# Whole-slot low parts, half-slot high parts, and a seventh Strassen-like slot in the first pair of the down product

## The chip, the cores and the metric

The kernel runs on one core of a Trainium2 chip. The metric is the device time of one execution in microseconds, from three runs of the kernel before; the profile is of one further execution. Four engines matter: PE (TensorE) multiplies, ACT (ScalarE) copies and rounds, DVE (VectorE) adds and subtracts, and SP (SyncE) only issues transfers from DRAM.

## The reference, cut to what matters

A decoder block on 256 tokens of width 2048, all in float32: a norm, one wide projection, two kinds of attention, two gates, an output projection, and a gated MLP with a short causal convolution.

```python
proj = rmsnorm(x, attn_norm_w) @ w_in                  # 2048 x 11264 columns
merged = sigmoid(g_ret) * (o_ret @ w_ret_up) + sigmoid(g_moba) * (o_moba @ w_moba_up)
x = x + merged @ w_out                                 # the kernel's x2
up = causal_dwconv(rmsnorm(x, ffn_norm_w) @ w_ffn_up)  # 2048 x 11264
a, b = split(up, 2)
x = x + (silu(a) * b) @ w_ffn_down                     # 5632 x 2048
return rmsnorm(x, final_norm_w)
```

## The kernel before

All weights come from DRAM once, cut into halves of 128 x 1024 float32 (512 KB). Two halves make a slot, and the kernel walks through 252 slots: those of the projection, 64 of the gates and the output projection (`middle_slots`), 88 of FFN's first product (`up`), 44 of its second (`down_slots`, "dn"), the last in two pairs of 22.

Precision is kept by splitting. Of each raw half (`raw`), ACT writes the high part `whi` (rounded to float32r), and DVE the low part `wlo = raw - whi`. A product is then three matmuls: high by high, high by low, low by high (`mm3`). The activations are split in the same way: `xb` holds those of the projection and of `up` (its tiles `xtiles`), `ot*`, `mg*`, `gh`/`gl` those of later products. In the projection's q and k groups and in `up`, the weights are the stationary operand (`wide_products`: per slot 16 matmuls of `whi` against 512 columns, then of `wlo` against 256). Elsewhere the activations are stationary and the 512 columns of weights move.

A "seven" is a slot whose 2 x 2 block product is done with seven block products in place of eight (the scheme of Strassen and Winograd): 21 matmuls of 512 columns in place of 24. It costs DVE and ACT more: four sums of raw weights and three more blocks to split (`seven_parts`, `seven_parts_apart`; tiles `tt`, `th`, `tl`, `t`), and four sums of activations, split too (`seven_sums`; tiles `room`, `s`), which both pairs of `dn` share. `SEVEN` lists which of the 22 slots in each pair of `dn` are sevens.

The order on each engine is the order of the program text: nothing is reordered, and a tool puts in the semaphores. In each slot's code first stands `part` for the next slot (ACT and DVE split it, then SP is told to load into the raw buffers that this frees), then small tasks (`run_tasks`: attention, convolution, norms), then the slot's matmuls. `RAW_BUFS` and `PART_BUFS` say how many halves of raw and of split weights fit: four each, so the splits run at most about a slot ahead of PE, and the loads two.

Of the kernel before, what the change touches and what calls it, by code (L numbers as in the profile page):

```python
# [16 lines left out]
P = 128  # L17
# [16 lines left out]
RAW_BUFS, PART_BUFS = 4, 4  # L34
# [45 lines left out]
SEVEN = ((4, 7, 10, 13, 16, 18), (3, 5, 7, 9, 12, 14, 16))  # L80
# [45 lines left out]
def block(ctx: ExitStack, tc: tile.TileContext, a):  # L126
# [32 lines left out]
    def spans(n):  # L159
        step = CW if n < 1 else 2 * CW  # L160
        return [slice(c, c + step) for c in range(0, 2 * CW, step)]

    def load(n, *some):
        if n < n_halves:
            if n not in raws:
                raws[n] = wp.tile([P, 2 * CW], F32, name="raw", bufs=RAW_BUFS)
            for w in some or spans(n):
                nc.sync.dma_start(raws[n][:, w], wts[order[n], :, w])

    def part(n, *some):  # L170

        if n < n_halves:
            if n not in parts:
                parts[n] = [wp.tile([P, 2 * CW], F32R, name=x, bufs=PART_BUFS) for x in ("whi", "wlo")]
            for w in some or spans(n):
                split2(parts[n][0][:, w], parts[n][1][:, w], raws[n][:, w])
            if not some or some[0] == spans(n)[-1]:
                raws.pop(n)
                load(n + RAW_BUFS)


# [14 lines left out]
    def mm3(out, ah, al, bh, bl, start, stop, **kw):  # L196
        mm(out, ah, bh, start=start, stop=False, **kw)
        mm(out, ah, bl, start=False, stop=False, **kw)
        mm(out, al, bh, start=False, stop=stop, **kw)

# [72 lines left out]
    xtiles = [px.tile([P, 2, 2, S], F32R, name=f"xb{i}", bufs=1) for i in range(KD // 2)]  # L273
# [18 lines left out]
    def part_x(k):  # L292
        for j in range(k, min(k + 2, KD)):
            split2(xh[j], xl[j], xts[j // 4][:, j % 4, :], vec[:, V_ATTN + j:V_ATTN + j + 1])
            if k == 0:
                part(0, spans(0)[j])
# [230 lines left out]
    def ffn(acc, f):  # L527

        pf = big["pf"]
        u = big["u"][f % 2]  # L530
        y = pf.tile([P, 2, S], F32, name="y", bufs=2)
# [12 lines left out]
        g = pf.tile([P, S], F32, name="g", bufs=2)  # L544
# [5 lines left out]
    def finish(acc, t, more):  # L550
# [17 lines left out]
        wf = big["wf"][1][:, CW:]  # L568
# [48 lines left out]
    def closed(kind, n, acc, more):  # L617
# [17 lines left out]
        elif kind == "up":  # L635
            if n == 0:
                assert not tasks, len(tasks)
                left.close()
                pf = big["pf"] = pool(left, "pf")
                big["gh"], big["gl"] = (pf.tile([P, NFB - 16, S], F32R, name="g" + x) for x in "hl")  # L640
                big["u"] = [pf.tile([P, 2, S + 2], F32, name=f"u{i}") for i in range(2)]
                for u in big["u"]:
                    nc.vector.memset(u[:, :, 0:2], 0.0)
# [12 lines left out]
    load(0)  # L656
# [8 lines left out]
    part(1)  # L665
# [12 lines left out]
    def seven_parts(n):  # L678


        r, q = raws.pop(n), raws.pop(n + 1)
        b11, b21, b12, b22 = r[:, :CW], r[:, CW:], q[:, :CW], q[:, CW:]
        (h1, l1), (h2, l2) = [[wp.tile([P, 2 * CW], F32R, name=x, bufs=PART_BUFS) for x in ("whi", "wlo")]
                              for _ in range(2)]
        (h3, l3), t2 = big["t14"], big["t2"]
        nc.scalar.activation(h1, r, AF.Copy)
        nc.scalar.activation(h2[:, CW:], b22, AF.Copy)
        nc.vector.tensor_sub(l1, r, f32(h1))
        nc.vector.tensor_sub(l2[:, CW:], b22, f32(h2[:, CW:]))
        nc.vector.tensor_sub(b11, b12, b11)  # L690
        nc.vector.tensor_sub(b12, b22, b12)
        nc.scalar.activation(h2[:, :CW], b12, AF.Copy)
        nc.vector.tensor_sub(b22, b22, b11)
        nc.scalar.activation(t2[:, 0, :], b22, AF.Copy)
        nc.vector.tensor_sub(b21, b21, b22)
        nc.scalar.activation(h3, r, AF.Copy)
        nc.vector.tensor_sub(l2[:, :CW], b12, f32(h2[:, :CW]))
        nc.vector.tensor_sub(t2[:, 1, :], b22, f32(t2[:, 0, :]))
        nc.vector.tensor_sub(l3, r, f32(h3))
        parts[n], parts[n + 1] = (h1, l1), (h2, l2)  # L700
        for i in (0, 1):
            load(n + i + RAW_BUFS)

    def seven_parts_apart(n, tt=None, t124=None):

        r, q = raws.pop(n), raws.pop(n + 1)
        b11, b21, b12, b22 = r[:, :CW], r[:, CW:], q[:, :CW], q[:, CW:]
        (h1, l1), (h2, l2) = [[wp.tile([P, 2 * CW], F32R, name=x, bufs=PART_BUFS) for x in ("whi", "wlo")]
                              for _ in range(2)]
        if t124 is None:  # L710
            splits = [(big["th"], big["tl"], big["tt"])]
            tt = [big["tt"][:, x, :] for x in range(3)]
        else:
            splits = [(*t124[x], tt[x]) for x in (1, 0, 2)]
        nc.vector.tensor_sub(tt[0], b12, b11)
        nc.vector.tensor_sub(b12, b22, b12)
        nc.vector.tensor_sub(tt[1], b22, tt[0])
        nc.vector.tensor_sub(tt[2], b21, tt[1])
        split2(h1, l1, r)
        split2(h2, l2, q)  # L720
        for hi, lo, full in splits:
            split2(hi, lo, full)
        parts[n], parts[n + 1] = (h1, l1), (h2, l2)
        for i in (0, 1):
            load(n + i + RAW_BUFS)
# [16 lines left out]
    def seven_sums(k, pool_k, tag, kind="dn"):  # L742
# [7 lines left out]
        nc.vector.tensor_sub(sums[:, 2, :], x[:, 0, :P], x[:, 0, P:])  # L750
        nc.vector.tensor_sub(sums[:, 1, :], sums[:, 0, :], x[:, 0, :P])
        nc.vector.tensor_sub(sums[:, 3, :], x[:, 1, :P], sums[:, 1, :])  # L752
        big["s", kind, k] = pool_k.tile([P, 2, 4, P], F32R, name=f"s{k}", tag=tag, bufs=1)
        hi, lo = big["s", kind, k][:, 0], big["s", kind, k][:, 1]
# [3 lines left out]
    def seven_products(xs, sums, t124, accs, halves):  # L758
# [94 lines left out]
    def middle_slots(slot):  # L853
# [4 lines left out]
        t124 = [two_of(p1.tile([P, 2, CW], F32R, name="t", tag="kq", bufs=4)) for _ in range(3)]  # L858
        for i, (seven, two) in enumerate(slots):
# [18 lines left out]
            if out and q == 3:  # L878
                right.close()
                pr = pool(right, "pr", "right")  # L880
                big["x2"] = pr.tile([P, NT, D], F32, name="x2")
# [19 lines left out]
            if i == 8:  # L901
                middle_pool()
                t124 = [[big[x][:, i, :] for x in ("th", "tl")] for i in range(3)]
            n = 2 * (slot + 1)
            if q == 0 and seven:
                times(r, sr)
            if i + 1 < len(slots) and slots[i + 1][0]:
                if i < 8:
                    tt = [p1.tile([P, CW], F32, name="tt", tag=x, bufs=2) for x in ("tmp", "tmp", "full")]
                    seven_parts_apart(n, tt, t124)  # L910
                else:
                    seven_parts_apart(n)
            else:
                part(n)
                part(n + 1)
# [9 lines left out]
            if not out:  # L925
                if c == 1 and q == 2:
                    seven_sums(3, big["pm"], "s3", "gr")
                if c == D // CW - 1 and q >= 10:
                    seven_sums(q - 10, big["pm"], f"s{q - 8}", "wo")
# [17 lines left out]
            halves = [parts.pop(2 * slot + h) for h in range(2)]  # L947
# [27 lines left out]
    def weighted(c, n):  # L975
        x3 = big["x2"][:, :, c * CW:(c + n) * CW]
        wf = big["wf"][c // 2][:, c % 2 * CW:(c % 2 + n) * CW]
        nc.vector.tensor_mul(x3, x3, wf[:, None, :].to_broadcast([P, NT, n * CW]))  # L978

    def down_slots(slot):  # L980
# [4 lines left out]
        t124 = [[x[:, :CW] for x in big["t14"]], [big["t2"][:, x, :] for x in range(2)],  # L985
                [x[:, CW:] for x in big["t14"]]]
        for i, (seven, where) in enumerate(slots):
# [8 lines left out]
            n = 2 * (slot + 1)  # L996
            if i + 1 < len(slots):
                if not slots[i + 1][0]:
                    part(n)
                    part(n + 1)  # L1000
                elif p == 0:
                    seven_parts(n)
                else:
                    seven_parts_apart(n, [big["pf"].tile([P, CW], F32, name="tt", tag=x, bufs=b)
                                          for x, b in (("u0", 1), ("u1", 1), ("y", 2))], t124)
            if p == 0 and q in SEVEN[0][:-1]:
                k = SEVEN[0].index(q) + 1
                seven_sums(k, px, f"xb{k % 5}")
            if p == 1 and q == 5:
                seven_sums(6, big["pf"], "wa")  # L1010
            if q == SEVEN[p][-1] + 1:
                v = big["pf"].tile([P, 2, S], F32, name="y", bufs=2).rearrange("p a t -> p (a t)")
                spawn(gathered, at, 2 * p, v)
            if p == 1 and q in (16, 17):
                j = q - 16
                wf = px.tile([P, 2 * CW], F32, name="wf", tag=f"xb{j + 1}", bufs=1)
                big.setdefault("wf", []).append(wf)
# [175 lines left out]
```

## Time and profile before

| what | value |
|---|---|
| median of 3 runs | 1417.61 us (1417.16 to 1417.9) |
| profiled execution, first to last instruction | 1415.7 us |
| what lies around it in a run | about 1.9 us |
| PE | 7215 matmul records, busy 99% of the span |
| DVE | busy 78% |
| ACT | busy 55% |
| DRAM read | 272.86 MB, 194 GB/s |

In the profile's groups a row has the source line, the engine, what is written and read with its shape, the number of instructions, the busy time in us and the mean of one in ns, and then the idle time just before them and what ended it. A PE record is longer (about 390 ns) than the distance to the next one, since matmuls overlap in the array; the distance is what counts. In a row of a timeline the first number is the start, the second how long the merged piece lasted.

### The profile page before, as it was taken

What the parts mean: (1) busy time and instruction counts of PE and PEld (TensorE: products, weight loads), DVE (VectorE), ACT (ScalarE), POOL (GpSimd) and SP (SyncE); (2) the same over time, 40 slices, a digit from 0 to 9 for tenths busy, and PEclk for the clock granted to TensorE, in tenths of its full rate; (3) what the DMA queues carried; (4) which work ended last, traced back from release to release, by engine and by line L of the source; (5) the groups of instructions that cost most, each with busy time, mean ns of one, the idle gap of its engine ahead of it and who ended that gap; (6) DMA issues with size and microseconds to landing.
All of it is one profiled execution on the core that took longest, in us unless ns stands there. A gap on an engine that the chain in (4) does not pass through costs nothing. (4 is left out here: it accounts for less than half of the span.)

```text
span 1415.7 us, 19297 instructions
## 1 busy us (share of the span) xinstructions
PE 1405.6 (99%) x7215; PEld 1202.7 (85%) x7215; DVE 1103.4 (78%) x1512; ACT 776.9 (55%) x1043; POOL 5.6 (0%) x14
## 2 busy tenths in 40 slices
PE   9999999999999999999999999999999999999997
PEld 7888888888888888888888888888888888888886
DVE  6687656867888989798677777777777778998886
ACT  6555454545556555555565555555555555555553
POOL 0000000000000000000000000000000000000000
PEclk9999999999999999999999999999999999999999
DMA  8755555555656656577555656556556555657664
GB/s 296 260 187 168 167 186 172 178 179 172 212 182 209 195 191 209 180 236 238 167 190 188 197 181 193 194 182 194 191 182 196 189 179 178 207 180 236 191 217 160
DMA packets 77325, 276.22 MB, mean 195 GB/s; under 512 B 8720, under 2 KB 9776, under 8 KB 77232
## 3 DMA queue, kind: packets, MB, share of 16 engines
q1 hardware_dynamic: 76800, 274.20, 60.1%
q8 instruction: 56, 0.92, 0.3%
q10 hardware_dynamic: 432, 0.79, 0.2%
q14 instruction: 37, 0.30, 0.1%
HBM read 272.86 MB, written 2.10 MB: 194 GB/s over the span
## 5 line engine op out<-in xcount | busy, mean ns | idle before, releaser
L186 DVE TENSOR_TENSOR wlo<-raw,whi 128x1024 fp32r<-128x1024 f32 (+1 forms) x493 | 584.1, 1219 | 234.7 <-ACT whi L185 108.8
L185 ACT ACTIVATE whi<-raw 128x1024 fp32r<-128x1024 f32 (+1 forms) x493 | 514.5, 1058 | 458.9 <-PE acc L194 247.9
L194 PE MATMUL acc<-xb,whi 128*128 128x512 f32 x1920 | 466.0, 392 | 1.1 <-ACT whi L185 1.1
L194 PEld LDWEIGHTS acc<-xb,whi 128*128 128x128 f32 x1920 | 350.6, 188 | 68.6 <-ACT whi L185 2.1
L194 PEld LDWEIGHTS acc<-xb,wlo 128*128 128x128 f32 x1920 | 250.9, 191 | 12.2
L194 PE MATMUL acc<-xb,wlo 128*128 128x256 f32 x1920 | 254.6, 282 | 0.0
L194 PE MATMUL acc<-whi,xb 128*128 128x512 f32 x572 | 183.3, 391 | 0.0
L194 PEld LDWEIGHTS acc<-whi,xb 128*128 128x128 f32 x572 | 107.4, 188 | 22.1
L194 PE MATMUL acc<-wlo,xb 128*128 128x512 f32 x286 | 111.5, 390 | 0.0
L194 PE MATMUL acc<-wlo,gh 128*128 128x512 f32 (+1 forms) x226 | 87.5, 387 | 0.0
L194 PE MATMUL acc<-whi,gl 128*128 128x512 f32 (+1 forms) x226 | 87.5, 387 | 0.0
L194 PE MATMUL acc<-whi,gh 128*128 128x512 f32 (+1 forms) x226 | 87.5, 387 | 0.0
L541 DVE SCALAR_TENSOR_TENSOR y<-u,vec,y 128x256 f32<-128x256 f32 x176 | 73.5, 479 | 0.0
L194 PEld LDWEIGHTS acc<-wlo,xb 128*128 128x128 f32 x286 | 53.7, 188 | 10.6
L194 PE MATMUL z<-whi,xb 128*128 128x512 f32 x156 | 51.9, 390 | 0.0
L194 PEld LDWEIGHTS acc<-wlo,gh 128*128 128x128 f32 x226 | 42.4, 188 | 8.8
L194 PEld LDWEIGHTS acc<-whi,gh 128*128 128x128 f32 x226 | 42.4, 188 | 8.7
L194 PEld LDWEIGHTS acc<-whi,gl 128*128 128x128 f32 x226 | 42.4, 188 | 8.6
L538 ACT ACTIVATE y<-u,vec 128x256 f32<-128x256 f32 x88 | 47.7, 590 | 0.0
L194 PEld LDWEIGHTS z<-whi,xb 128*128 128x128 f32 x156 | 29.3, 188 | 6.1
L755 ACT ACTIVATE s<-room 128x512 fp32r<-128x512 f32 x13 | 8.2, 633 | 44.7 <-DVE room L752 44.7
L534 DVE TENSOR_TENSOR u<-y,r2b 128x512 f32<-128x512 f32 x44 | 30.5, 693 | 1.5
(304 smaller groups left out, 1593.1 us busy)
## 6 DMA issues: line engine op xcount, KB each, us to landing
raw<-in_wts SPq DMA_DIRECT2D x503, 512.0 KB, 4.3
rows<-in_x SPq DMA_DIRECT2D x4, 512.0 KB, 7.7
x<-in_x SPq DMA_DIRECT2D x4, 512.0 KB, 6.1
xt<-in_xT SPq DMA_DIRECT2D x3, 512.0 KB, 7.0
wf<-in_wf SPq DMA_DIRECT2D x2, 512.0 KB, 7.1
out<-x SPq DMA_DIRECT2D x4, 256.0 KB, 2.5
out<-x ACTq DMA_DIRECT2D x2, 384.0 KB, 3.3
xt<-in_xT SPq DMA_DIRECT2D x2, 256.0 KB, 4.4
```

Of the source, the lines that this page charges most:

```text
L185: nc.scalar.activation(hi, full, AF.Copy)
L186: nc.vector.tensor_sub(lo, full, f32(hi))
L194: to.append(lambda: nc.tensor.matmul(out, a, b, **kw))
L534: nc.vector.tensor_mul(u[:, :, 2:], y, twice(big["r2b"]))
L538: nc.scalar.activation(y[:, j, :], u[:, j, 0:S], AF.Identity, scale=cv[j][:, 0:1], bias=cv[j][:, 3:4])
L541: nc.vector.scalar_tensor_tensor(y[:, j, :], u[:, j, i:i + S], cv[j][:, i:i + 1], y[:, j, :], op0=OP.mult, op1=OP.add)
L755: nc.scalar.activation(hi, sums, AF.Copy)
```

## The change

Seven things change.

1. Raw and split weights are held by slots (128 x 2048), two of each, in the same memory. ACT still writes `whi` by halves, but DVE writes `wlo` of the whole slot in one subtraction, and both loads of a slot are issued behind it. In the first four slots the old halves stay (`part_of`).
2. The products of a slot are put in another order (`all3`): all that need `whi` first, those that need `wlo` last.
3. The sevens take their sums from the other corner of the blocks, so that the first half is untouched, and split the three extra blocks in one subtraction of 128 x 1536 in `dn` too.
4. `SEVEN[0]` has seven slots in place of six: (5, 7, 9, 11, 13, 15, 17) for (4, 7, 10, 13, 16, 18). The matmuls of 512 columns fall from 4989 to 4986.
5. `x2` (2 MB) is written to the output's DRAM in the slots of `up` with n = 2 and read back in slots 1, 3, 5 and 7 of `dn`, each time in four pieces of 512 KB.
6. Its room in SBUF then holds the activation sums 0 to 4 for `dn`, made in `up` (n = 8, 14, 20, 26, 32) and no longer in `dn`'s first pair; sums 5 and 6 are made in slots 6 and 10 of `dn`.
7. The final norm's weights `wf` are loaded in one piece of 1 MB in slot 11 of `dn`'s second pair, before in two of 512 KB in slots 16 and 17.

```diff
-RAW_BUFS, PART_BUFS = 4, 4
+RAW_BUFS, PART_BUFS = 2, 2
-SEVEN = ((4, 7, 10, 13, 16, 18), (3, 5, 7, 9, 12, 14, 16))
+SEVEN = ((5, 7, 9, 11, 13, 15, 17), (3, 5, 7, 9, 12, 14, 16))
+SUMS_IN_UP = (8, 14, 20, 26, 32)
...
+    def loads(s):
+        raws.pop(s)
+        for h in range(2):
+            load(2 * (s + RAW_BUFS) + h)
...
+    def part(s):
+        if 2 * s < n_halves:
+            hi, lo = parts[s] = part_tiles()
+            for h in range(2):
+                w = slice(2 * CW * h, 2 * CW * (h + 1))
+                nc.scalar.activation(hi[:, w], raws[s][:, w], AF.Copy)
+            nc.vector.tensor_sub(lo, raws[s], f32(hi))
+            loads(s)
...
+    def all3(products):
+        for bank, edges, ah, al, bh, bl in products:
+            for x in (ah, al):
+                begin, end = edges(1)
+                mm(bank, x, bh, start=begin, stop=end, to=stream)
+        for bank, edges, ah, al, bh, bl in products:
+            begin, end = edges(1)
+            mm(bank, ah, bl, start=begin, stop=end, to=stream)
...
+    def seven_parts(s, tt, th, tl):
+        r = raws[s]
+        b11, b21, b12, b22 = [r[:, x * CW:(x + 1) * CW] for x in range(4)]
+        hi, lo = parts[s] = part_tiles()
+        nc.vector.tensor_sub(tt[0], b22, b21)
+        nc.vector.tensor_sub(b22, b22, b12)
+        nc.vector.tensor_sub(tt[1], b12, tt[0])
+        nc.vector.tensor_sub(tt[2], b11, tt[1])
+        for h in range(2):
+            w = slice(2 * CW * h, 2 * CW * (h + 1))
+            nc.scalar.activation(hi[:, w], r[:, w], AF.Copy)
...
+            nc.scalar.activation(th, full, AF.Copy)
+            nc.vector.tensor_sub(lo, r, f32(hi))
+            nc.vector.tensor_sub(tl, full, f32(th))
+        loads(s)
...
+            if p == 0 and q in (1, 3, 5, 7):
+                if q == 1:
+                    big["x2"] = px.tile([P, NT, D], F32, name="x2", tag="xb0", bufs=1)
+                w = slice(q // 2 % 2 * 2 * CW, (q // 2 % 2 + 1) * 2 * CW)
+                nc.sync.dma_start(big["x2"][:, q // 4, w], orows[:, q // 4, w])
+            if p == 0 and q == 6:
+                seven_sums(5, sums_tile(px, "xb1"))
+            if p == 0 and q == 10:
+                big["room"] = two_of(pair(big["uy"][:, 4 * S + 4:4 * S + 4 + 2 * CW]))
+                seven_sums(6, sums_tile(big["pf"], "wb"))
...
+            if p == 1 and q == 11:
+                big["wf"] = big["pr"].tile([P, NT, D], F32, name="wf", tag="x2", bufs=1)[:, 0, :]
+                nc.sync.dma_start(big["wf"], a["wf"][None, :].to_broadcast([P, D]))
...
+            if kind == "up" and n == 2:
+                w = slice(kc % 2 * 2 * CW, (kc % 2 + 1) * 2 * CW)
+                nc.sync.dma_start(orows[:, kc // 2, w], big["x2"][:, kc // 2, w])
+            if kind == "up" and n in SUMS_IN_UP and kc == 1:
+                k = SUMS_IN_UP.index(n)
+                if k == 0:
+                    big["s"] = big["pr"].tile([P, 4, 2, 4, P], F32R, name="s", tag="x2", bufs=1)
+                    big["room"] = two_of(big["pf"].tile([P, 2, CW], F32, name="room", tag="wb", bufs=1))
+                seven_sums(k, big["s"][:, k] if k < 4 else sums_tile(big["pf"], "wa"))
```

How the instructions move at three places:

DVE in the first pair of `dn`, before: the end of one slot, a seven, the split of a plain slot, and the activation sums for a later seven (`raw`, `t` weights; `room`, `s` activation sums).

```order
L186 TENSOR_TENSOR wlo<-raw,whi 128x1024 x2
L186 TENSOR_TENSOR gl<-g,gh 128x256
L688 TENSOR_TENSOR wlo<-raw,whi 128x1024
L689 TENSOR_TENSOR wlo<-raw,whi 128x512
L690 TENSOR_TENSOR raw<-raw 128x512
L691 TENSOR_TENSOR raw<-raw 128x512
L693 TENSOR_TENSOR raw<-raw 128x512
L695 TENSOR_TENSOR raw<-raw 128x512
L697 TENSOR_TENSOR wlo<-raw,whi 128x512
L698 TENSOR_TENSOR t_10483<-raw,t_10483 128x512
L699 TENSOR_TENSOR t_10482<-raw,t_10481 128x1024
L186 TENSOR_TENSOR wlo<-raw,whi 128x1024 x2
```

The next six rows there are sums of activations (L748 to L752, L756). DVE at the same place now, two sevens with a plain slot between them (`uy` is one tile that also holds the weight sums):

```order
L197 TENSOR_TENSOR wlo<-raw,whi 128x2048
L731 TENSOR_TENSOR uy<-raw 128x512
L732 TENSOR_TENSOR raw<-raw 128x512
L733 TENSOR_TENSOR uy<-raw,uy 128x512
L734 TENSOR_TENSOR uy<-raw,uy 128x512
L747 TENSOR_TENSOR wlo<-raw,whi 128x2048
L748 TENSOR_TENSOR t<-uy,t 128x1536
L197 TENSOR_TENSOR wlo<-raw,whi 128x2048
```

A seven is six DVE instructions in place of nine, its sums stand ahead of both low parts, and the activation sums stand here in two slots only.

DVE at the start of `up`, before: the last splits of x2's activations (L189), the low parts of `up`'s first slot, and x2's last sums (L851).

```order
L189 SCALAR_TENSOR_TENSOR xb_80<-acc,vec,xb_80 128x256 x2
L189 SCALAR_TENSOR_TENSOR xb_81<-acc,vec,xb_81 128x256 x2
L186 TENSOR_TENSOR wlo<-raw,whi 128x1024 x2
L851 TENSOR_TENSOR x_5325<-z,x_5325 128x512 x4
L186 TENSOR_TENSOR wlo<-raw,whi 128x1024 x4
```

DVE at the start of `up` now:

```order
L211 SCALAR_TENSOR_TENSOR xb_78<-acc,vec,xb_78 128x256 x8
L197 TENSOR_TENSOR wlo<-raw,whi 128x2048
L879 TENSOR_TENSOR x_4890<-z,x_4890 128x512 x4
L197 TENSOR_TENSOR wlo<-raw,whi 128x2048 x2
```

The two low halves of the first slot, each of which waited for its own high half, are one instruction that waits for both.

PE in a seven of `dn`, before (`ot*`, `gh`, `gl` activations, `s` their sums, `t` the extra weight blocks):

```order
L194 MATMUL acc_10616<-whi,otrh 128x512
L194 MATMUL acc_10616<-wlo,otrh 128x512
L194 MATMUL acc_10616<-whi,otrl 128x512
L194 MATMUL acc<-whi,otrh 128x512
L194 MATMUL acc<-wlo,otrh 128x512
L194 MATMUL acc<-whi,otrl 128x512
```

PE in a seven of `dn` now:

```order
L216 MATMUL acc_9710<-whi,otmh 128x512
L216 MATMUL acc_9710<-whi,otml 128x512
L216 MATMUL acc<-whi,otmh 128x512
L216 MATMUL acc<-whi,otml 128x512
L216 MATMUL acc<-whi,s 128x512 x2
L216 MATMUL acc_9711<-whi,s 128x512 x2
L216 MATMUL acc_9710<-t,s 128x512 x2
L216 MATMUL acc_9711<-t,s 128x512 x2
L216 MATMUL acc<-t,otmh 128x512
L216 MATMUL acc<-t,otml 128x512
L216 MATMUL acc_9710<-wlo,otmh 128x512
L216 MATMUL acc<-wlo,otmh 128x512
```

The low part of the weights, read by the second matmul of a seven before, is read by the fifteenth now.

More of the change, by code (lines that the diff above doesn't have):

```diff
@@ L157, in block, with raw, part_tiles, part_of @@
     order += [at_half["dn", c] + k for _, two in down() for k, c in two]
-    def spans(n):
-        step = CW if n < 1 else 2 * CW
-        return [slice(c, c + step) for c in range(0, 2 * CW, step)]
+    def raw(s):
+        if s not in raws:
+            raws[s] = wp.tile([P, 4 * CW], F32, name="raw", bufs=RAW_BUFS)
+        return raws[s]
     def load(n, *some):
         if n < n_halves:
[L165 to L179, printed above, removed]
+            w0 = n % 2 * 2 * CW
+            for w in some or (slice(0, 2 * CW),):
+                nc.sync.dma_start(raw(n // 2)[:, w0 + w.start:w0 + w.stop], wts[order[n], :, w])
+    def loads(s):
+        raws.pop(s)
+        for h in range(2):
+            load(2 * (s + RAW_BUFS) + h)
+    def part_tiles():
+        return [wp.tile([P, 4 * CW], F32R, name=x, bufs=PART_BUFS) for x in ("whi", "wlo")]
+    def part_of(s, w, last=False):
+        if 2 * s < n_halves:
+            if s not in parts:
+                parts[s] = part_tiles()
+            split2(*(x[:, w] for x in parts[s]), raws[s][:, w])
+            if last:
+                loads(s)
+    def part(s):
+        if 2 * s < n_halves:
+            hi, lo = parts[s] = part_tiles()
[4 more added lines that the diff above has]
+            loads(s)
+    def halves_of(s):
+        hi, lo = parts.pop(s)
+        return [[x[:, 2 * CW * h:2 * CW * (h + 1)] for x in (hi, lo)] for h in range(2)]
     def split2(hi, lo, full, scale=None):
@@ L655, in block @@
     load_x(0, 2)
-    load(0)
+    load(0, slice(0, CW), slice(CW, 2 * CW))
     load_x(2, 2)
@@ L664, in block @@
     part_x(2)
-    part(1)
+    part_of(0, slice(2 * CW, 4 * CW), True)
     load_x(12)
@@ L704, in seven_parts_apart @@
[L704 to L712, printed above, removed]
-        else:
[L714 to L725, printed above, removed]
+    def seven_parts(s, tt, th, tl):
[9 more added lines that the diff above has]
+            nc.scalar.activation(hi[:, w], r[:, w], AF.Copy)
+        if isinstance(th, list):
+            for x, y in zip(th, tt):
+                nc.scalar.activation(x, y, AF.Copy)
+            nc.vector.tensor_sub(lo, r, f32(hi))
+            for x, y, z in zip(tl, tt, th):
+                nc.vector.tensor_sub(x, y, f32(z))
+        else:
+            full = tt[3]
+            nc.scalar.activation(th, full, AF.Copy)
+            nc.vector.tensor_sub(lo, r, f32(hi))
+            nc.vector.tensor_sub(tl, full, f32(th))
+        loads(s)
@@ L727, in two_blocks, with three @@
+    def three(tile, w=CW):
+        return [tile[:, x, :] for x in range(3)]
     def two_blocks(k, kind="dn"):
@@ L902, in middle_slots @@
                 middle_pool()
-                t124 = [[big[x][:, i, :] for x in ("th", "tl")] for i in range(3)]
-            n = 2 * (slot + 1)
+                th, tl = big["th"], big["tl"]
+                t124 = list(zip(three(th), three(tl)))
             if q == 0 and seven:
@@ L946, in middle_slots @@
             run_tasks()
-            halves = [parts.pop(2 * slot + h) for h in range(2)]
+            halves = halves_of(slot)
             if seven:
@@ L1027, in down_slots @@
                 weighted(2, 1)
-            halves = [parts.pop(2 * slot + h) for h in range(2)]
+            halves = halves_of(slot)
             if seven:
@@ L1062, in down_slots, with products @@
                     spawn(added, tiles[0][d], d)
-    def products(kind, n, act, accs, kc, halves, tokens, nk):
+    def products(kind, n, act, accs, kc, halves, counts, nk):
         if len(accs) == 4:
-            if kind == "up" and n > 0:
-                wide_products(accs, 4 * kc, halves, nk, range(4))
-            elif slot < 3:
+            if slot < 3:
                 for h in range(2):
@@ L1072, in products @@
             else:
-                for blocks in ((0, 1), (2, 3)):
+                for blocks in (range(4),) if kind == "up" and n > 0 else ((0, 1), (2, 3)):
                     wide_products(accs, 4 * kc, halves, nk, blocks)
             return
+        some = []
         for h, (hi, lo) in enumerate(halves):
```

160 lines of the change are left out of this document (69 added, 91 removed).

## The prediction

> **What bounds the kernel now.** I read the page's busy times first, then the waits of PE, then PE's own timeline.
>
> ```profile
> span 1415.7 us, 19297 instructions
> PE 1405.6 (99%) x7215; PEld 1202.7 (85%) x7215; DVE 1103.4 (78%) x1512; ACT 776.9 (55%) x1043; POOL 5.6 (0%) x14
> PE   9999999999999999999999999999999999999997
> DVE  6687656867888989798677777777777778998886
> ```
>
> ```profile
> PE idle L651 <- DVE idle L648: 1.2, 1, 1.2
> PE acc L194 <- ACT whi L185: 1.1, 1, 1.1
> PEld acc L194 <- DVE t L699: 0.4, 1, 0.4
> ```
>
> PE is busy in every slice. All its waits together are under 3 us: the start (1.2), the second half of the first slot (1.1), and one wait of its weight loads (PEld) for a seven's extra blocks (0.4). So the kernel lasts as long as PE's list of matmuls. What shortens DVE, ACT or DRAM work alone gains nothing; what makes one of them late costs all of the lateness beyond the lead that the splits have on PE. The price of a matmul comes from the timeline, here in the first pair of `dn`:
>
> ```profile
> 1218.78 0.39 PE L194 MATMUL acc<-whi,gh 128*128 128x512 f32 x1
> 1219.00 0.39 PE L194 MATMUL acc<-wlo,gh 128*128 128x512 f32 x1
> 1219.23 0.39 PE L194 MATMUL acc<-whi,gl 128*128 128x512 f32 x1
> 1219.45 0.39 PE L194 MATMUL acc<-whi,gh 128*128 128x512 f32 x1
> ```
>
> From start to start it is 0.22 to 0.23 us (0.67 over three; the eight from 684.37 to 686.18 further down take 0.226 each; I use 0.227), with the same stationary block (the first two) as with another. A plain slot is thus 24 x 0.227 = 5.45 us, a seven 21 x 0.227 = 4.77 us, a pair of them 10.2 us.
>
> The other prices, by form:
>
> ```profile
> L186 DVE TENSOR_TENSOR wlo<-raw,whi 128x1024 fp32r<-128x1024 f32 x491 | 582.7, 1221 | 234.6 <-ACT whi L185 108.8 <-PE acc L194 71.7 <-issue 53.1
> L185 ACT ACTIVATE whi<-raw 128x1024 fp32r<-128x1024 f32 x491 | 513.3, 1059 | 458.9 <-PE acc L194 247.9 <-issue 111.0 <-DVE raw L716 38.1
> L186 DVE TENSOR_TENSOR tl<-tt,th 128x1536 fp32r<-128x1536 f32 x16 | 28.0, 1752 | 0.2 <-ACT th L185 0.2
> L185 ACT ACTIVATE th<-tt 128x1536 fp32r<-128x1536 f32 x16 | 23.8, 1489 | 2.5 <-DVE tt L718 2.4
> L715 DVE TENSOR_TENSOR tt<-raw 128x512 f32<-128x512 f32 x25 | 17.2, 687 | 6.5 <-DMA raw<-in_wts 5.3 <-DVE wlo L186 1.1
> ```
>
> No subtraction of 2048 columns is shown. The step from 1024 to 1536 is 0.53 us, so 1.75 + 0.53 = 2.28 us is my estimate; two of 1024 (2.44) bound it above, four thirds of 1.752 (2.34) differ little.
>
> **The change part by part.**
>
> *Three matmuls fewer* in the first pair of `dn`: 3 x 0.227 = 0.68 us, all on PE. [...]
>
> *The wait of 0.4 us* for `t` (L699, a line of `seven_parts` and so of `dn`'s first pair) goes whole or stays: 0 to 0.4, I take 0.2.
>
> *The new order of products.* It loads the stationary block for every matmul, as before (PE and PEld both have 7215). The rows above show the same 0.227 with and without a change of block: 0. The low part is now needed at a slot's 17th matmul, 3.6 us in (15th in a seven, 3.2 us).
>
> *Whole-slot low parts.* DVE saves 2.44 - 2.28 = 0.16 us in nearly 250 slots, some 39 us, which is worth nothing by itself (PE is the bound). The cost is that the low part waits for both high halves, and that both loads wait for it. It bites where PE takes the low part early and the high part is late, in `wide_products`. One such place is the first slot of `up`; its ACT, DVE and PE rows:
>
> ```profile
> 682.45 3.89 ACT L185 ACTIVATE whi<-raw 128x1024 fp32r<-128x1024 f32 x4
> 683.53 2.36 DVE L186 TENSOR_TENSOR wlo<-raw,whi 128x1024 fp32r<-128x1024 f32 x2 [0.46 <-ACT whi L185]
> 684.37 1.98 PE L194 MATMUL acc<-xb,whi 128*128 128x512 f32 x8
> 686.18 1.11 PE L194 MATMUL acc<-xb,wlo 128*128 128x256 f32 x8
> ```
>
> The second high half ends two fourths into ACT's 3.89, at 684.4. Before, the first low half was done at 684.75; now the whole one starts at 684.45 and ends at 686.75, and PE asks at 686.18: 0.6 us of new stall (0 if ACT comes earlier, 0.6 at most). I take 0.6. Late next are x2's four sums and the low part of `up`'s second slot, each a third of a microsecond; they have slots to spare.
>
> *Loads in pairs.* A load of 512 KB and a pair of them, 1.1 us apart, in the trace:
>
> ```profile
> raw<-in_wts SPq DMA_DIRECT2D x503, 512.0 KB, 4.3
> L168 SPq DMA_DIRECT2D raw<-in_wts x2: 328/328/328, 649.2 to 650.3; - x2
> DMA to landing us min/median/max: 3.5/4.0/4.4
> ```
>
> The second lands 1.1 + 4.4 = 5.5 us after the first's issue. Issued directly one after the other it should be 4.4 to 5.5; I take 5.2. At the start, the first half of the third slot was loaded early, and now waits for the second:
>
> ```profile
> 7.22 4.27 SPq L168 DMA_DIRECT2D raw<-in_wts  x2
> 15.29 1.06 ACT L185 ACTIVATE whi<-raw 128x1024 fp32r<-128x1024 f32 x1 [0.29 <-DMA raw<-in_wts]
> 18.41 2.00 PE L194 MATMUL acc<-xb,whi 128*128 128x512 f32 x8
> ```
>
> Issued at 7.22 it landed at 15.3, 8 us later, since DRAM's queue was full; issued at 11.2 (where the second was) plus 4.3 it lands at 15.5 and PE needs its high part at 18.4: 0. If it came a full 3.9 us later, 1.9 us of stall.
>
> *The first pair of `dn`* is the place that decides. The busy times of gates, `up` and this stretch:
>
> ```profile
> core 0: us, PE busy (x) PEld busy (x) DVE busy (x) ACT busy (x) POOL busy (x), PEclk, DMA share, GB/s
> 406.00:447.00 41.00, 41.00 (x181) 33.70 (x180) 39.08 (x45) 21.92 (x21) 0.00 (x0) 1.00 0.61 196
> 820.00:860.00 40.00, 40.00 (x232) 35.34 (x231) 29.73 (x43) 23.15 (x33) 0.00 (x0) 1.00 0.59 185
> 1208.00:1292.00 84.00, 84.00 (x371) 69.23 (x370) 76.19 (x103) 46.08 (x55) 0.00 (x0) 1.00 0.62 201
> ```
>
> DVE was at 76 of 84 us. A pair of seven and plain slot now costs it 4 x 0.69 + 2.28 + 1.75 + 2.28 = 9.1 us of 10.2, so it keeps up. But all seven sevens use the same raw buffer, and its loop is longer: sums 2.75, low part 2.28, loads 5.2 make 10.25 us (9.4 to 10.5 with loads of 4.4 to 5.5) against 10.2. Six rounds lose 0.3 us (nothing to 1.9). To that come the activation sums in slots 6 and 10:
>
> ```profile
> 1219.14 0.68 DVE L748 TENSOR_TENSOR room<-otrh,otrl 128x512 f32<-128x512 f32 x1
> 1221.57 0.69 DVE L756 TENSOR_TENSOR s<-room,s 128x512 fp32r<-128x512 f32 x1 [0.70 <-ACT s L755]
> ```
>
> From 1219.14 to 1222.26 they hold DVE 3.1 us; of each, 1.1 us fits into the pair's slack, 2.0 us is lost, 4.0 for both. The lead from which this is taken: a low part cannot start before PE has left the slot before (its buffer), say at 0; it ends at 2.3, the loads land at 7.5, and a seven's high part is ready 2 x 0.69 + 1.06 = 2.5 us later, at 10.0. PE needs it three slots after 0, at 5.45 + 4.77 + 5.45 = 15.7. Lead 5.7 us, use 4.3: no stall at my values; at the upper bound 5.9, a stall of 0.2. The landings of single loads in this stretch:
>
> ```profile
> DMA to landing us min/median/max: 3.5/4.6/6.3
> ```
>
> The longest took 6.3 us; a whole series of pairs at 6.0 would give 6 x 0.85 + 4.0 - 5.7 = 3.4 us. I take 0.
>
> *The gates* (first windows row): the 39 of 41 us that DVE worked fall by 8 x 0.16. The loop has only four rounds: 0.
>
> *x2's trips and `wf`.* Four pieces of 512 KB, one per slot, raise the share of the DMA engines in `up` from 0.59 to 0.59 x 1.5 = 0.89: not full. A piece ahead of a load delays it by what the second of a pair waits, 5.5 - 3.5 = 2.0 us, under the lead of 5.7; `wf` by twice that, 4. In `dn`, the pieces of slots 5 and 7 fall into the series of sevens, but behind its loads. Nobody waits for them: x2 is wanted after the last seven. The sums moved into `up` take 3.1 us of DVE every third group there, which is idle a quarter of the time. 0 for all, 2 us if a piece meets the worst of the series.
>
> The end (`finish`) is unchanged.
>
> Sum: - 0.68 - 0.2 + 0.6 = - 0.3 us on the profiled 1415.7, so 1415.4 there; the runs' median lies 1.9 us above it, thus **1417.3 us**.
>
> **The rivals.** What a run here can tell from no change is 0.2%, 2.8 us.
>
> *The series of sevens starves PE* (slower). The price is above: nothing until loads take 5.4 us, and 3.4 us at 6.0; for + 2.8 us over all they must take about 6.0 from first issue to second landing in every round. For it speak the 6.3 us seen here; against it the 4.4 of the quoted pair, and that loads now come less often together. Time 1418 to 1421. [...]
>
> *Small stalls elsewhere*, each under a microsecond: the third slot's loads (up to 1.9), other `wide_products` slots, gates after their activation sums. Two of them give 1418 to 1419.5: still no change.
>
> *DVE's relief pays*. If PE lost time to late operands all along, 39 us less on DVE would show. The waits of PE above hold 2.7 us; with the three matmuls and the waits after the start (1.1 + 0.4) gone, the best is 1415.4. Beyond 2.8 us I find nothing.
>
> *x2's read collides* with the series: 2 us more on the first rival, 1419 to 1423.
>
> **How the numbers follow.** Forecast (1416 to 1418): 0.58. Small stalls, 1418 to 1419.5: 0.20. The series starves: 0.12, half of it beyond 1420.4. Collision of x2 with it: 0.06, most of it beyond. DVE's relief: 0.04, at most half of it below 1414.8. Slower by over 0.2% is then 0.06 + 0.05 + 0.03 for what I have not seen = 0.14, faster 0.03, the rest 0.83. The range goes from the best case to where the starving series has most of its weight: 1415.4 to 1420.8.
>
> **What would show it.** PE rows in the first pair of `dn` 0.227 us apart through all sevens, no wait of PE for `raw`, `whi` or `t` there: the lead held. A wait for ACT or DVE in its later sevens (slots 13 to 17), with DVE waiting for DMA before L731: the first rival. A gap of 0.6 us before the first `wlo` of `up`: the whole-slot price. DVE's subtraction of 2048 at 2.28 us, total some 40 us lower. A pair's second landing at 5.2. The forecast is wrong if PE's records lie further apart than 0.227 in the new order, or if the transfers of x2 hold up a load by more than 5 us.

## The result, and the profile after

The changed kernel takes 1431.47 us (median of four runs, 1429.91 to 1432.16), the kernel before beside it 1417.65 (1417.16 to 1417.90). The ratio is 1.0098 with a 95% interval of 1.0083 to 1.0112: 13.8 us slower. Forecast were 1417.3 us and a range of 1415.4 to 1420.8; the time lies 10.7 us above the range.

The profiled execution of the changed kernel, first lines of its page (busy time of each engine, then two rows of the span in 40 slices):

```profile
span 1430.4 us, 18545 instructions
PE 1410.8 (99%) x7212; PEld 1203.6 (84%) x7212; DVE 1085.8 (76%) x1243; ACT 758.0 (53%) x1018; POOL 5.6 (0%) x14
PE   9999999999999999999999999999999999999997
DVE  6587656866888879788677878777777777887877
```

At this grain nothing has happened: PE is as full as before, has its three matmuls fewer, and DVE works 17.6 us less. The list of what PE waited for tells more (engine, line waited at, what it waited for: us in total, times, longest; the start's 1.2 us are left out):

```profile
PE acc L216 <- ACT whi L196: 2.4, 1, 2.4
PE acc L216 <- DVE mfull L410: 2.2, 3, 1.1
PE acc L216 <- ACT gate L673: 1.6, 1, 1.6
PE acc L216 <- ACT whi L207: 1.2, 1, 1.2
PE acc L216 <- DVE wlo L197: 0.9, 1, 0.9
PE acc L244 <- issue: 0.8, 1, 0.8
PE z L216 <- DVE mgl L208: 0.6, 1, 0.6
PE acc L216 <- DVE rfull L410: 0.5, 2, 0.3
```

Before, two waits of PE were over 0.5 us, both at the start. Now nine are, and four more lie between 0.2 and 0.5, most of them for causes that were not in that list. `mfull` and `rfull` are the sums that empty PE's accumulators after a group of `mqk` or `rqk`; `gate` is `rg`'s silu, which empties one too; `mgl` is a split of the gated activations. Only `whi` and `wlo` are weights. The row with "issue" belongs to DVE too: L244 transposes x2 at the end of `wo`, and starts 0.1 us behind DVE's last sum of x2.

Waits do not hold all of it, so I counted another way: the distance from each matmul's start to the next, less 0.227 us (512 columns), 0.120 (256) or 0.110 (128), close to their median distances in both kernels (0.227, 0.120 and 0.109), summed over stretches of the matmul list. The idle matmuls at the start are left out; the time from the last of them to the first real one is in the first row. All figures in us, one profiled execution each; the kernels of the right columns come below.

| stretch | before | changed | sums_behind | low_halves | both | mended | whole_late | low_next |
|---|---|---|---|---|---|---|---|---|
| start (first 20 us) | 2.1 | 2.6 | 3.1 | 1.8 | 1.9 | 1.6 | 2.0 | 2.8 |
| rest of the first groups | 1.2 | 5.3 | 4.1 | 2.3 | 3.1 | 1.9 | 1.5 | 7.1 |
| end of `rg` 1 | 0.0 | 1.9 | 2.0 | 0.8 | 0.7 | 0.0 | 0.8 | 3.5 |
| gates and `wo` | 0.8 | 3.0 | 3.3 | 0.7 | 0.7 | 0.7 | 0.7 | 10.5 |
| first slots of `up` | 0.1 | 1.3 | 1.3 | 0.1 | 0.1 | 0.1 | 0.1 | 1.3 |
| rest of `up` | 1.3 | 1.3 | 1.3 | 1.3 | 1.3 | 1.3 | 1.3 | 1.3 |
| first pair of `dn` | 0.2 | 5.2 | 0.4 | 5.3 | 0.4 | 0.4 | 0.4 | 11.6 |
| second pair of `dn` | 0.1 | 0.4 | 0.4 | 0.4 | 0.4 | 0.4 | 0.4 | 2.0 |
| sum | 5.7 | 21.0 | 15.8 | 12.6 | 8.5 | 6.4 | 7.1 | 40.0 |
| matmuls at their price | 1396.7 | 1396.0 | 1396.0 | 1396.0 | 1396.0 | 1396.0 | 1396.0 | 1396.0 |

From before to changed that is - 0.7 + 15.3 = 14.6 us, and the two spans are 14.7 apart: the account is complete. The loss has two parts, 5 us in the first pair of `dn` and some 10 us spread over places ahead of `up`'s second group.

*A small place.* The end of the group `mqk` 2. DVE's timeline of the changed kernel (start, duration, engine, line, what it writes and reads), and PE's row after it:

```profile
72.63 2.27 DVE L197 TENSOR_TENSOR wlo<-raw,whi 128x2048 fp32r<-128x2048 f32 x1
74.83 0.67 DVE L208 TENSOR_TENSOR mkq<-mfull,mkq 128x512 fp32r<-128x512 f32 x1
75.43 1.39 DVE L211 SCALAR_TENSOR_TENSOR vl<-vfull,r,vh 128x512 fp32r<-128x512 f32 x2
76.75 1.48 DVE L410 TENSOR_TENSOR mfull<-acc,mfull 128x512 f32<-128x512 f32 x2
77.48 1.19 PE L216 MATMUL acc<-xb,whi 128*128 128x512 f32 x4 [0.60 <-DVE mfull L410]
```

The same place in the kernel before, whose PE asked for this accumulator at 74.82:

```profile
69.35 2.34 DVE L186 TENSOR_TENSOR wlo<-raw,whi 128x1024 fp32r<-128x1024 f32 x2
71.62 0.67 DVE L186 TENSOR_TENSOR mkq<-mfull,mkq 128x512 fp32r<-128x512 f32 x1
72.23 1.40 DVE L189 SCALAR_TENSOR_TENSOR vl<-vfull,r,vh 128x512 fp32r<-128x512 f32 x2
73.55 0.67 DVE L365 TENSOR_TENSOR mfull<-acc,mfull 128x512 f32<-128x512 f32 x1
```

DVE has the same row of work in the same order and no pause. Before, the first sum ended at 74.22, 0.60 ahead of PE. Now the first of the two ends at 77.43, and PE had wanted it at 76.71. The 1.3 us were lost two slots earlier: there the low part had to wait for its second high half and ended 0.5 us behind its slot's start on PE, before 0.9 ahead of it, and DVE, busy without a pause from the next low part on, carried that along. The low parts themselves are used in time; it is the work queued behind them that comes late.

*The large place.* Slot 12 of `dn`, right behind the activation sums issued at slot 10. ACT, DVE and PE of the changed kernel:

```profile
1245.21 1.49 ACT L746 ACTIVATE t<-uy 128x1536 fp32r<-128x1536 f32 x1 [0.35 <-DVE uy L734]
1250.78 0.63 ACT L785 ACTIVATE s<-uy 128x512 fp32r<-128x512 f32 x1 [4.08 <-DVE uy L782]
1251.32 1.99 ACT L196 ACTIVATE whi<-raw 128x1024 fp32r<-128x1024 f32 x2
1247.21 1.75 DVE L748 TENSOR_TENSOR t<-uy,t 128x1536 fp32r<-128x1536 f32 x1
1250.45 0.29 DVE L782 TENSOR_TENSOR uy<-uy 128x128 f32<-128x128 f32 x1
1249.63 0.39 PE L216 MATMUL acc<-t,otrh 128*128 128x512 f32 x1
1252.41 0.77 PE L216 MATMUL acc<-whi,gh 128*128 128x512 f32 x1 [2.39 <-ACT whi L196]
```

ACT stood idle for 4.08 us before L785, the high part of the sums. It waited for DVE, which still had a low part and `t` to make before it came to the sums. Behind L785 in ACT's queue stood the high parts of slot 12 (L196), though that slot's raw weights had landed at 1245.7 and ACT was free from 1246.7. PE waited. And PE lost more than the wait: the eight matmuls behind it stand 0.427 us apart. The granted clock, in windows around that place (the column PEclk is the third from the end):

```profile
core 0: us, PE busy (x) PEld busy (x) DVE busy (x) ACT busy (x) POOL busy (x), PEclk, DMA share, GB/s
1249.60:1252.40 2.80, 0.42 (x2) 0.00 (x0) 1.77 (x6) 1.62 (x3) 0.00 (x0) 1.00 0.64 260
1252.40:1256.00 3.60, 3.59 (x9) 2.88 (x10) 2.66 (x2) 1.85 (x2) 0.00 (x0) 0.53 0.00 0
1256.00:1260.00 4.00, 4.00 (x19) 3.31 (x18) 3.93 (x5) 2.66 (x3) 0.00 (x0) 1.00 0.79 252
```

### The profile page after: what moved, and what is told of

Same layout as the page of the kernel before. It is cut to its first block, busy times and chain, and to the rows that moved or that the text cites. A ratio compares the mean times of both kernels' runs of the same rounds, so it can differ in the third digit from the quotient of the medians.

```text
span 1430.4 us, 18545 instructions
## 1 busy us (share of the span) xinstructions
PE 1410.8 (99%) x7212; PEld 1203.6 (84%) x7212; DVE 1085.8 (76%) x1243; ACT 758.0 (53%) x1018; POOL 5.6 (0%) x14
## 4 chain that ended last, share of the span: by engine, by line
PE 88%; DVE 6%; ACT 2%; DMA 2%; issue 1%; SPq 0%; DVEq 0%; POOLq 0%; POOL 0%; ACTq 0%
PE acc L216 76%; PE z L216 10%; DVE wlo L197 3%; ACT whi L196 2%; DMA raw<-in_wts 2%; PE o L216 0%; PE s L216 0%; DVE wlo L747 0%; PE rs L216 0%; PE z L244 0%; DVE wlo L208 0%; DVE room L778 0%; PE acc L244 0%; DVE vl L211 0%; PE pt L244 0%
## 5 line engine op out<-in xcount | busy, mean ns | idle before, releaser
L197 DVE TENSOR_TENSOR wlo<-raw,whi 128x2048 fp32r<-128x2048 f32 x216 | 494.7, 2290 | 268.7 <-ACT whi L196 263.9
L196 ACT ACTIVATE whi<-raw 128x1024 fp32r<-128x1024 f32 x432 | 434.2, 1051 | 361.2 <-PE acc L216 252.0
L216 PE MATMUL acc<-xb,whi 128*128 128x512 f32 x1920 | 466.6, 392 | 2.1 <-ACT whi L207 1.2
L216 PEld LDWEIGHTS acc<-xb,whi 128*128 128x128 f32 x1920 | 350.9, 189 | 69.9 <-ACT whi L207 2.1
L216 PEld LDWEIGHTS acc<-xb,wlo 128*128 128x128 f32 x1920 | 250.8, 191 | 13.5 <-DVE wlo L197 1.3
L216 PE MATMUL acc<-xb,wlo 128*128 128x256 f32 x1920 | 254.7, 283 | 0.9 <-DVE wlo L197 0.9
L216 PE MATMUL acc<-whi,xb 128*128 128x512 f32 x572 | 141.9, 392 | 3.5 <-ACT gate L673 1.6
L737 ACT ACTIVATE whi<-raw 128x1024 fp32r<-128x1024 f32 x64 | 67.7, 1060 | 114.1 <-DVE raw L732 48.6
L216 PEld LDWEIGHTS acc<-whi,xb 128*128 128x128 f32 x572 | 106.1, 188 | 25.8 <-ACT gate L673 2.0
L216 PE MATMUL acc<-whi,gh 128*128 128x512 f32 (+1 forms) x226 | 88.7, 393 | 2.4 <-ACT whi L196 2.4
L216 PE MATMUL acc<-whi,gl 128*128 128x512 f32 (+1 forms) x226 | 88.4, 391 | 0.0
L216 PE MATMUL acc<-wlo,xb 128*128 128x512 f32 x286 | 73.5, 390 | 0.0
L585 DVE SCALAR_TENSOR_TENSOR uy<-uy,vec 128x256 f32<-128x256 f32 x176 | 73.3, 479 | 0.0
L747 DVE TENSOR_TENSOR wlo<-raw,whi 128x2048 fp32r<-128x2048 f32 x30 | 68.6, 2285 | 0.5 <-ACT whi L737 0.5
L216 PEld LDWEIGHTS acc<-wlo,xb 128*128 128x128 f32 x286 | 53.7, 188 | 11.4
L216 PE MATMUL acc<-wlo,gh 128*128 128x512 f32 (+1 forms) x226 | 58.0, 387 | 0.0
L216 PEld LDWEIGHTS acc<-whi,gh 128*128 128x128 f32 x226 | 43.1, 191 | 12.1 <-ACT whi L196 3.1
L216 PEld LDWEIGHTS acc<-whi,gl 128*128 128x128 f32 x226 | 43.0, 190 | 8.8
L216 PEld LDWEIGHTS acc<-wlo,gh 128*128 128x128 f32 x226 | 42.5, 188 | 8.7
L582 ACT ACTIVATE uy<-uy,vec 128x256 f32<-128x256 f32 x88 | 47.6, 588 | 2.1 <-DVE uy L578 2.1
L216 PE MATMUL z<-whi,xb 128*128 128x512 f32 x156 | 39.6, 389 | 0.0
L216 PEld LDWEIGHTS z<-whi,xb 128*128 128x128 f32 x156 | 29.3, 188 | 6.1
```

The source lines that it names most:

```text
L196: nc.scalar.activation(hi[:, w], raws[s][:, w], AF.Copy)
L197: nc.vector.tensor_sub(lo, raws[s], f32(hi))
L216: to.append(lambda: nc.tensor.matmul(out, a, b, **kw))
L582: nc.scalar.activation(y[:, j, :], u[:, j, 0:S], AF.Identity, scale=cv[j][:, 0:1], bias=cv[j][:, 3:4])
L585: nc.vector.scalar_tensor_tensor(y[:, j, :], u[:, j, i:i + S], cv[j][:, i:i + 1], y[:, j, :], op0=OP.mult, op1=OP.add)
L737: nc.scalar.activation(hi[:, w], r[:, w], AF.Copy)
```

## The experiments

My theory, from these views: nothing is short of time on any engine; what is late stands in a queue behind something that waits (called *queues*). Two edits should then bring back nearly all, each its own places. The main rival: two whole-slot buffers, loaded again only when a whole slot is split, make the loads late.

**sums_behind**: the changed kernel with the activation sums' split behind the next slot's high parts, in `dn` alone.

```diff
-        nc.scalar.activation(hi, sums, AF.Copy)
-        nc.vector.tensor_sub(lo, sums, f32(hi))
+        later.append(split)            # the same two instructions
...
# down_slots, behind the next slot's part() or seven_parts():
+            while held_back:
+                held_back.pop()()
```

> The changed kernel with one edit: in the first pair of dn, the high and low part of the two activation sums (slots 6 and 10) are issued after the next slot's high parts instead of ahead of them. Theory (queues): in slot 10, ACT stood idle for 4.1 us before the sums' high part, which waited for DVE's sums, while the next slot's weights had already landed; PE then waited 2.55 us for that slot's high part, and eight matmuls after it took 0.427 instead of 0.227 us, with a gap of 0.34 before: 4.3 us in all. These go: 1427.2 (1426.5 to 1428). Rival (DVE is simply too busy in the series of sevens, or the loads too late): the stall stays or moves to the next slots, over 1430.

Measured: 1427.49 us (ratio to before 1.0070, 1.0055 to 1.0085), 4.0 below the changed kernel. ACT at the same place:

```profile
1243.12 1.99 ACT L196 ACTIVATE whi<-raw 128x1024 fp32r<-128x1024 f32 x2
1247.30 0.63 ACT L787 ACTIVATE s<-uy 128x512 fp32r<-128x512 f32 x1 [2.19 <-DVE uy L782]
```

The high parts now go first and are done at 1245.1, 3.4 us before PE wants them. The stretch falls from 5.2 to 0.4, and what changes elsewhere lies in the first groups. DVE's busy time (1085.8 us) and the loads' median (4.4 us) are those of the changed kernel. Late loads there are in both: in slots 11, 15 and 17 DVE waits for one before it can start a seven, 1.58, 1.24 and 1.54 us in the changed kernel, 1.06, 1.22 and 1.50 here. Without the wait in ACT's queue they cost PE nothing.

**low_halves**: the changed kernel with the low part in two instructions.

```diff
-                nc.scalar.activation(hi[:, w], raws[s][:, w], AF.Copy)
-            nc.vector.tensor_sub(lo, raws[s], f32(hi))
+                split2(hi[:, w], lo[:, w], raws[s][:, w])
```

> The changed kernel with one edit: the low part of a plain slot is made in two instructions of 1024, each right behind its own half's high part, instead of one of 2048 behind both. Tiles, loads, product order and the first pair of dn stay. Theory (queues): the one low part ends 1.07 us later than two halves would, and what stands behind it on DVE is late by that: the sums that free PE's banks after mqk and rqk (4.07 us of stall in five places, 3.7 back), the sums ahead of the gate of rg 1 (1.9, 1.1 back), three stalls in the gates and wo (2.2, 1.8 back), the first low part of up (1.1, all back). 1423.8 (1422.5 to 1425.5), with the 2.55 us stall in dn still there. Rival (two slots of buffers, loaded only when a whole slot is done, make the loads late): the stalls stay, 1430 to 1432, and DVE works 35 us more.

Measured: 1422.12 us (1.0033, 1.0020 to 1.0046), 9.4 below the changed kernel, with 15.5 us more work for DVE (1101.3 against 1085.8). That is less than the 35 I had put down from the durations of single instructions: two in a row overlap, and take 2.34 us from start to end, as the row at 69.35 above shows, against 2.27 of the one. The waits of PE that are left:

```profile
PE acc L215 <- ACT whi L206: 3.0, 3, 2.4
PE acc L215 <- ACT gate L672: 0.4, 1, 0.4
PE acc L215 <- ACT t L745: 0.3, 1, 0.3
PE acc L215 <- DVE mfull L409: 0.2, 1, 0.2
```

`rfull`, `mgl` and `wlo` are gone, `mfull` fell from 2.2 to 0.2, and the 2.4 us of slot 12 stayed, as they should. The gain is 1.7 above my 7.7. In the table it is 8.4: 3.0 in the first groups, 2.3 in the gates, 1.2 in `up`, 1.1 at `rg`, 0.8 at the start, of which I had left out the last and half a microsecond of the gates, while the first groups gave 0.7 less than I had put down. The table's kernels are single executions, and those of **low_halves** scatter from 1419.8 to 1423.7, which covers the 1.0 between the table and the medians.

Tiles and the order of products are those of the changed kernel, and a slot is still loaded only when all of it is split; its loads can go out up to 1.07 us sooner, behind the shorter second subtraction. Does that explain the gain? In the changed kernel a transfer was waited for ahead of four of the nine late places: weights for 1.15 us at the end of the first group, 0.45 ahead of `mgl` and 2.47 at the end of `wo`; and rows of x, on which ACT waited 4.02 us ahead of the small place shown above. At the last three the waits are here too (0.46, 2.34 and 4.50 us), and PE loses 0.1 us or less there. So the rival of the loads falls, but for the end of the first group (below).

**both**: the two edits together.

> Both edits at once: sums behind the next high parts in dn, and low parts in two instructions of 1024. Theory (queues): the two gains add up, 4.3 + 7.7 = 12.0 us: 1419.5 (1418 to 1421.5). Rival (loads late, or DVE too busy in the sevens): over 1427.

Measured: 1418.23 us (1.0006, 0.9997 to 1.0015). The gains add up: 4.0 + 9.4 = 13.4 expected from the parts, 13.2 found. The change is back to where it had been forecast, without a measurable difference from the kernel before.

**low_next**: the new order of products undone.

```diff
-            for x in (ah, al):
-                mm(bank, x, bh, ...)
-        for bank, edges, ah, al, bh, bl in products:
-            mm(bank, ah, bl, ...)
+            for x, y in ((ah, bh), (al, bh), (ah, bl)):
+                mm(bank, x, y, ...)
```

> The changed kernel with the new order of products undone: each product issues its three matmuls together again, so the first low part of a slot's weights is used 0.45 us after the slot starts instead of two thirds through. Theory (queues): the new order is what gives the whole-slot low part its time; without it the seven-product slots of dn, the gates and the first slots of mv, rv, rg wait for it in some places: 2 to 8 us slower than the changed kernel, 1433 to 1439. Rival (the new order itself costs time, by the order of weights and banks at PE): faster, 1418 to 1428. My forecast had put the order at 0.

Measured: 1447.79 us (1.0210, 1.0193 to 1.0227), 16.3 slower than the changed kernel: the direction of the theory, and twice the upper end of what I gave. The first row of PE's waits:

```profile
PE acc L216 <- DVE wlo L197: 10.8, 10, 2.5
```

Ten waits for a whole-slot low part, and two of them (2.0 and 2.7 us, in `dn`) were followed by 8 and 14 matmuls at half the clock, which I had not counted in. So the new order is not a detail: with whole-slot low parts, 16.3 us hang on it.

**whole_late**: whole-slot low parts only from the second group of `up` on, two instructions ahead of it, the sums behind.

> The changed kernel with the sums behind the next high parts in dn, and with low parts in two instructions only for the slots ahead of the second group of up; from there on one whole-slot low part as in the changed kernel. Theory (queues): in up and dn nothing that PE waits for stands behind the low part on DVE, so the whole-slot form costs nothing there, and its saving of DVE time brings nothing: as 'both', 1418.2 (1417.2 to 1419.5). Rival (the whole-slot form costs wherever it stands): 1420 or more.

Measured: 1418.30 us (before beside it 1417.15; 1.0008, 0.9999 to 1.0017). **both** stood at 1.0006 of the kernel before beside it (1417.53), so the two are alike within what the runs can tell. 114 low parts are made whole here:

```profile
L201 DVE TENSOR_TENSOR wlo<-raw,whi 128x2048 fp32r<-128x2048 f32 x114 | 261.2, 2291 | 144.0 <-ACT whi L197 140.7
```

They cost nothing and bring nothing that shows (0.5 us between the two ratios, less than the width of either interval). It is not the large instruction that is dear here, but the large instruction where something that PE waits for stands behind it.

**mended**: **both**, and the last two waits taken away.

```diff
 # part_of, at the start: each half is loaded again as soon as it is split
-            if last:
-                loads(s)
+            if w.stop % (2 * CW) == 0:
+                raws[s + RAW_BUFS] = raws[s]
+                load(2 * (s + RAW_BUFS) + w.stop // (2 * CW) - 1)
 # rg 1, last slot: the sums' split is issued behind closed(), so behind the gate's silu
```

> The kernel 'both' with its two remaining waits taken away: at the start the third and later slots' halves are loaded as soon as the same half of the buffer is free (before: only when the whole slot was split), and in rg 1 the high and low part of the last activation sum are issued behind the gate's silu instead of ahead of it. Theory (queues): in 'both' PE still waited 1.36 and 0.37 us at the end of the first group and at the start for loads that came late, and 0.58 us for the gate; these go: 1418.2 - 2.0 = 1416.2 (1415.6 to 1417.2), 0.1% faster than before, by the three matmuls fewer and the shorter wait at the start. Rival (there is a price of whole-slot buffers that I have not found): 1418 or more.

Measured: 1417.35 us (before beside it 1417.15; 1.0001, 0.9992 to 1.0010). The waits are gone; PE's list is down to the start and 0.3 us for POOL:

```profile
PE idle L701 <- DVE idle L698: 1.2, 1, 1.2
PE across L218 <- POOL r L282: 0.3, 1, 0.3
```

Against the kernel before beside each, **both** was 0.7 us slower and **mended** is 0.2 slower: a gain of 0.5 that the intervals do not tell from none, and not the 2.0 I had given. (The 0.9 between the bare medians holds 0.4 by which the kernel before was quicker in these later runs.) I had taken the 2.0 from the profiled execution of **both**, which was its longest run (1419.65, median 1418.23): the wait for late loads at the end of the first group (1.36 us there) is 0.4 in **low_halves** and missing in **whole_late**. It varies from one execution to the next. No version that I tried beats the kernel before: the three matmuls are 0.7 us, and that is less than the runs can tell.

**stall_12** and **stall_17** ask about the slow matmuls: **sums_behind**, with 12 or 17 copies put on ACT ahead of slot 12's high parts.

> The kernel 'sums_behind' (no stall at slot 12 of dn) with 12 copies of 128x512 put on ACT ahead of slot 12's first high part, some 0.56 us each; the copies are extra work and change no result. PE should stand still for 12 x 0.56 - 4.3 = 2.4 us there. Theory (the clock follows the stall): eight or so matmuls after it at 0.427 us, as after the 2.55 us stall. Rival (the slow matmuls have another cause, the sums or the loads): all at 0.227.

> As stall_12, with 17 copies: PE stands still for 17 x 0.56 - 4.3 = 5.2 us. If the number of slow matmuls grows with the stall, some 16 at 0.427 us; if it is a fixed time of recovery, 8 to 14 as after 2.55 and 2.71 us. Rival (another cause): all at 0.227.

A copy took 0.66 us (12 in 7.91), where 0.56 had been my estimate, so the stalls came out at 3.57 and 8.08 us. Windows of the stall and what follows, first of stall_12, then of stall_17:

```profile
1248.70:1252.30 3.60, 0.43 (x2) 0.00 (x0) 0.00 (x0) 3.47 (x6) 0.00 (x0) 1.00 0.04 16
1252.30:1256.00 3.70, 3.47 (x9) 2.68 (x10) 2.54 (x2) 2.59 (x4) 0.00 (x0) 0.56 0.00 0
```

```profile
1250.30:1258.30 8.00, 0.38 (x2) 0.00 (x0) 0.22 (x1) 7.65 (x13) 0.00 (x0) 0.64 0.12 50
1258.30:1262.80 4.50, 4.21 (x10) 3.35 (x11) 3.29 (x3) 2.65 (x4) 0.00 (x0) 0.50 0.03 2
1262.80:1267.00 4.20, 4.20 (x19) 3.48 (x19) 4.13 (x5) 2.91 (x3) 0.00 (x0) 0.99 0.70 248
```

Eight slow matmuls after 3.57 us, ten after 8.08, where sums and loads had nothing to do with the stall. In these two the slow stretch came with the stall, and did not grow in step with it. Both runs are single executions.

## Why the prediction was wrong

By its own steps:

- *What bounds the kernel.* Right, and the sentence that carried it too: work taken off DVE brings nothing, lateness beyond the lead costs all of itself. DVE's 17.6 us less brought nothing, in **whole_late** too.
- *Three matmuls fewer*, - 0.68: the account has them at - 0.7, by their count and the price of 0.227, which is the median distance in both kernels. *The wait for `t`*, - 0.2: wrong, though small. It did not go; PE's weight loads now wait twice for the high part of `t`, 0.6 us in all (`PEld acc L216 <- ACT t L746: 0.6, 2, 0.4`).
- *The whole-slot low part in DVE's time*, 2.28: measured 2.290 (216 of them). The saving was sized wrongly: DVE works 17.6 us less, not some 39. Two subtractions of 1024 in a row take 2.34 us together, not 2.44; the row at 683.53 in the prediction shows 2.36. As PE is the bound, neither number matters for the time.
- *The first slot of `up`*, + 0.6: measured 1.0 and a slow restart of 0.1 (1.3 - 0.1 = 1.2 in the account). The right mechanism, and half the size.
- *A pair's second landing*, 5.2: over the 15 pairs of the first pair of `dn` the median is 4.95 (4.8 to 6.2). The loads, on which I had spent most of the argument, were not the trouble.
- *The first pair of `dn`*, taken as 0 with at most 3.4: measured + 5.0. **This step failed.** I counted the sums as 3.1 us of DVE each, 2.0 of it lost, and set them against a lead of 5.7 us. They also have an instruction on ACT, which waits for DVE's sums, and behind it on ACT stood the next slot's high parts, for which DVE's next low part waits in turn. From a seven's first sum on DVE (L731) to the next one's, with activation sums between, the changed kernel took 13.07 and 13.21 us: 2.9 and 3.0 over PE's 10.2 for the pair of slots. In **sums_behind**, with the same work in another order, it took 11.00 and 11.12. Of the 5.0 us, 1.7 are half clock, which was no part of my sum. The wait that I should have read stood on ACT, in the timeline of which I quoted DVE's rows:

```profile
1220.91 0.63 ACT L755 ACTIVATE s<-room 128x512 fp32r<-128x512 f32 x1 [3.32 <-DVE room L752]
1221.45 2.00 ACT L185 ACTIVATE whi<-raw 128x1024 fp32r<-128x1024 f32 x2
```

So the queue was there before too, and cost nothing: the high parts behind it were ready by 1223.4, and PE asked for them at 1224.2. In the changed kernel the first of the two sums (slot 6) still cost PE only 0.2 us; the second found the lead used up.

- *Gates, start and the other slots*, taken as 0, with a rival of two small stalls, each under a microsecond: measured + 9 us in some nine places of 0.4 to 1.9. **This is the other failure.** The rival had two kinds of place right, slots of `wide_products` and gates behind their activation sums. I had worked out one place, in `up`, where the late low part itself is used, and took it as the price of the whole-slot form. Everywhere else I asked whether the low part would be in time, which it was, and not what stands behind it on DVE: the sums that empty accumulators, the splits of `mg`, the sums that the gate's silu waits behind. **low_halves** shows it: the same tiles and the same late transfers, the low part 1.07 us earlier, and 9.4 us are back.
- *The new product order*, 0: right as to itself, wrong in what I thought of it. Without it the kernel is 16.3 us slower (**low_next**).
- *x2's trips and `wf`*, 0: right. "Rest of `up`" stands at 1.3 in both kernels, and in **both** the first pair of `dn` is at 0.4 with the same transfers.
- *The rivals.* None named the queue. The starving series has the right place, and part of its sign came, the waits for loads ahead of L731; but in **sums_behind** the same sums run with waits nearly as long and without a stall.

What stays open: the stall at the end of the first group varies between the profiled executions (0 to 1.7 us), and late loads stand ahead of it. It is missing in **mended**, which loads by halves there, but in **whole_late** too, which does not; whether loading by halves did anything, and what the gate brought, the runs do not tell.

## What to carry to other kernels

When an instruction gets longer or waits for more, list what is queued behind it on its engine at every kind of place it occurs, with the lead of each, not only when its own result is needed: here the result was in time nearly everywhere, and the work behind it cost 9 us. An operation that went from one engine to another and back (a sum on DVE, its split on ACT) held the second queue here while the first was busy, 4.08 us ahead of L785; issue the second half behind the work that is ready. And an engine that was relieved where it was not the bound gave nothing back here, as the 114 whole-slot instructions of **whole_late** show (1.0008 of the kernel before, **both** 1.0006).

## What the runs showed of the hardware

Some stalls of PE cost more here than themselves. In the changed kernel two of 1.36 and 1.79 us (ahead of the matmuls at 10.27 and 349.12) were followed by a distance of 0.34 us and then by 0.226 to 0.236, and the granted clock stayed at 1.00 (windows 10.30 to 20.00 and 349.20 to 356.00). Behind the stall of 2.55 us, at slot 12 of `dn`, eight matmuls stood some 0.427 us apart, and the granted clock was 0.50 from 1252.50 to 1255.80. In **low_next** 14 such matmuls followed a stall of 2.71 us and 8 one of 1.98, both in `dn` (granted clock 0.50 and 0.66):

```profile
1244.40:1250.40 6.00, 5.88 (x14) 4.63 (x15) 5.93 (x7) 2.54 (x2) 0.00 (x0) 0.50 0.77 263
1270.00:1275.00 5.00, 4.93 (x15) 3.89 (x16) 4.93 (x7) 2.54 (x2) 0.00 (x0) 0.66 0.63 210
```

The stalls of 3.57 and 8.08 us, in **stall_12** and **stall_17**, were followed by 8 and 10. At 0.427 in place of 0.227, 8 to 14 matmuls are 1.6 to 2.8 us on top of the stall.

The length alone does not part the two kinds: **low_next** had another stall of 2.00 us, at 55.8, and no slow stretch behind it, though the 1.98 in `dn` had one. What made the difference, no run here shows.
